# Hybrid encoder layer: attention weights left unscaled until the head pair is done, and the last linear-attention q and k columns computed as seven-product units

## The chip, the cores and the metric

One core of one Trainium2 chip. The metric is device time in microseconds (us) for one call of the layer, lower is better. The kernel before takes 2159.4 us, the median of three runs (2157.53 to 2160.07).

## What is computed

One layer over 512 tokens of width 2048, in float32. The parts that the change touches:

```
h = rmsnorm(x); proj = h @ w_in        # columns: aq ak av (1024 each), gq gk (512 each), gv gr (1024 each), 32 gate columns
# group A, 16 heads x 64: three (window, dilation) patterns, T5 bias, merged by their softmax denominators
logits = q @ k.T * 64**-0.5 + bias;  p = exp(logits - max);  s = sum(p);  o = p @ v / s
# group B, 4 heads, dk 128, dv 256: bidirectional gated linear attention on gq, gk, gv, then a norm and a swish gate gr
x = x + concat(A, B) @ w_out
x = x + (silu(h2 @ w_gate) * (h2 @ w_up)) @ w_down;  rmsnorm
```

At 512 tokens the three patterns and their merge are one softmax over all 512 keys, with a bias that holds the log of how many patterns reach a distance.

## The kernel before

Every large product is made in split precision: each operand is rounded to a `fp32r` high part (on ScalarE) and the remainder is kept as a low part (a subtraction on VectorE), and three matmuls are summed (high by high, high by low, low by high). There are two ways to do a product. A **job** (`run_job`, L311 on) does it plainly: 512 output columns, 16 slices of the contraction, and for each slice four PSUM banks by three 128x512 matmuls, twelve in all; kind "A" (L337 to L339) has the features on the partitions, kind "B" (L346 to L348) the tokens. A **unit** (`Feed.products`, `Front`) does 256 output columns in 2x2 blocks with seven block products instead of eight (the sums of blocks are made on VectorE). A unit has four pieces; a piece has seven products, and each of them two matmuls of 128x512 (L1562) and two of 128x256 (L1548). `evac7` then puts the seven results together with nine copies on ScalarE, seven additions of 256 columns and one of 512 on VectorE and four adding DMAs; `finish` multiplies by the row of reciprocal norms and writes to DRAM.

The program is written out in one order and each engine has its own queue, served strictly in that order. The order around the change:

1. Two jobs for the attention's v columns.
2. `Front`: 14 units, for the gate gr (4), the lower half of gq and gk (2), and the attention's q and k (8). q and k go to DRAM (`qkd`) and are read back per pair of heads by `read_qk` and rounded by `load_qk`.
3. Three jobs: job A for the upper half of gq and gk (`evac_gqk`, L849), then the two gv jobs.
4. Three half jobs of `w_out` (the rows that belong to attention), one whole job of `w_out`, then the rest of `w_out`, the SwiGLU units and the down projection.

In stages 3 and 4 the attention and then the gated linear attention (`gla`) run **beside** the jobs. They are generators in the list `side`. After each bank's three matmuls a job adds its rate (`RATES`, steps per slice) to a credit, and for each whole credit one step of the first generator in `side` is put into the program; `urgent` generators get one step before it. `attention` (L711) takes two steps for each unit u (a head's 128 queries; 64 units, 8 to a pair of heads). The first step of u has the scores of u (two matmuls, L630, L631) and the ScalarE work: the round of an earlier unit (L670) and the exponential of u-1 (L648), which also sums it. The second step has TensorE's transposes (L662), the products with v (L686, L687) every second unit, and on VectorE the remainder (L676), the bias and maximum of u (L640) and the sum of the two halves of the result (L705). Between the exponential and the transposes `att_norm` (L651, L653) takes the reciprocal of the sum on VectorE and scales the unit's 128x512 weights there for even u; `att_scale` (L657) does it on ScalarE for odd u. The result of a pair (`mixf`) is rounded (L738) and its remainder is taken (L751); the `w_out` half jobs read it as `mixh`.

PSUM has eight banks. The running job holds four; the scores, transposes and v products share the other four, and a bank is handed out again in the order in which it was given back (`Slots`, first in, first out), so a matmul that opens a bank waits for the VectorE instruction that read it last.

## Time and profile before

| | us |
|---|---|
| median of three runs | 2159.4 |
| the profiled execution | 2159.02 |
| its span in the profile | 2157.2 |
| stage 2, `Front`, 14 units (first L1562 to the first L337) | 104.2 to 378.0 |
| attention, first L630 to the last L687 | 399.0 to 609.8 |
| TensorE's granted clock | 1.00 of full speed |

In the profile's groups each line names engine, operation, tiles, count, busy time and the mean of one, and then the idle time of the engine just before these instructions with its releaser. PE is the matmul row of TensorE and PEld its weight loads. Matmuls overlap, so the distance between the starts of two of them says what one costs; its duration does not. In a timeline row the first number is the start, the second the length.

### The profile page before, as it was taken

The numbers are of one execution on the slowest core, as the hardware profiler recorded it, in microseconds if no ns is written. First come the engines' busy times: TensorE is split into PE (matmuls) and PEld (weight loads), VectorE is DVE, ScalarE is ACT, GpSimd is POOL, SyncE is SP. The second block draws the span as 40 slices with busy tenths as digits, with TensorE's granted clock in tenths as the row PEclk, the third lists the DMA queues.
The fourth block names the chain that finished last, engine by engine and source line by source line (L and its number), as shares of the span: only waits on it lengthen the run. The fifth ranks groups of instructions, "written<-read, shape, count | busy, mean of one in ns | idle before, by whom it ended". The sixth has DMA issues, their size and how long they took to land.

```text
span 2157.2 us, 35082 instructions
## 1 busy us (share of the span) xinstructions
PE 2145.5 (99%) x12714; PEld 1896.6 (88%) x12714; DVE 1843.6 (85%) x3187; ACT 1234.4 (57%) x2250; POOL 364.0 (17%) x501
## 2 busy tenths in 40 slices
PE   9999999999999999999999999999999999999998
PEld 7888888888888889888888888888888899999987
DVE  6699999688878788899999998999989888888885
ACT  8455555578876456455555555555555655555562
POOL 0011222211121110022112211221122220021300
PEclk9999999999999999999999999999999999999999
DMA  6367778846575863567677667776677885576982
GB/s 203 136 181 182 179 179 192 245 143 190 174 220 172 279 243 103 149 181 182 181 179 196 173 183 182 178 194 174 180 188 181 260 212 178 179 183 156 282 309 78
DMA packets 266203, 407.55 MB, mean 189 GB/s; under 512 B 19309, under 2 KB 163613, under 8 KB 266030
## 3 DMA queue, kind: packets, MB, share of 16 engines
q1 hardware_dynamic: 206238, 274.59, 39.8%
q0 software_dynamic: 59472, 130.19, 27.1%
q8 instruction: 100, 1.64, 0.3%
q14 instruction: 73, 0.60, 0.1%
q10 hardware_dynamic: 320, 0.53, 0.1%
HBM read 287.47 MB, written 66.39 MB: 164 GB/s over the span
## 4 chain that ended last, share of the span: by engine, by line
PE 56%; DMA 1%; issue 1%; DVE 1%; POOL 0%; ACT 0%; DVEq 0%; ACTq 0%; POOLq 0%
PE ps L1562 25%; PE ps L1548 12%; PE ps L1926 5%; PE ps L1927 5%; PE ps L1925 5%; PE ps L346 1%; PE ps L348 1%; PE ps L347 1%; PE ps L2122 1%; PE ps L2121 1%; PE ps L2120 1%; DMA gd<-b 1%; DMA b<-a 0%; POOL xd L1806 0%; DVE b L1471 0%
## 5 line engine op out<-in xcount | busy, mean ns | idle before, releaser
L1466 ACT CAST b<-b 128x1024 fp32r<-128x1024 f32 (+1 forms) x585 | 533.8, 944 | 386.4 <-DVE b L1471 193.1
L1471 DVE TENSOR_TENSOR b<-b,b 128x1024 fp32r<-128x1024 f32 (+1 forms) x585 | 614.0, 1084 | 34.4 <-ACT b L1466 22.9
L1562 PE MATMUL ps<-b,b 128*128 128x512 f32 x1708 | 500.7, 393 | 0.4 <-ACT b L1466 0.2
L1562 PE MATMUL ps<-a,b 128*128 128x512 f32 x1428 | 418.7, 393 | 0.3 <-DVE b L1582 0.2
L1562 PEld LDWEIGHTS ps<-b,b 128*128 128x128 f32 x1708 | 289.4, 188 | 32.6 <-ACT b L1466 0.6
L1548 PEld LDWEIGHTS ps<-b,b 128*128 128x128 f32 x1708 | 280.6, 190 | 40.8
L1548 PE MATMUL ps<-b,b 128*128 128x256 f32 x1708 | 307.4, 280 | 0.0
L1548 PEld LDWEIGHTS ps<-a,b 128*128 128x128 f32 x1428 | 236.9, 189 | 38.0 <-DVE b L1471 0.5
L1562 PEld LDWEIGHTS ps<-a,b 128*128 128x128 f32 x1428 | 238.5, 188 | 24.1 <-issue 0.6
L1548 PE MATMUL ps<-a,b 128*128 128x256 f32 x1428 | 256.6, 280 | 0.1
L1453 DVE TENSOR_TENSOR b<-b 128x512 f32<-128x512 f32 x268 | 183.6, 685 | 19.0 <-PE ps L1927 7.3
L1926 PE MATMUL ps<-b,b 128*128 128x256 f32 x624 | 176.6, 283 | 0.0
L1927 PE MATMUL ps<-b,b 128*128 128x256 f32 x624 | 176.6, 283 | 0.0
L1925 PE MATMUL ps<-b,b 128*128 128x256 f32 x624 | 176.6, 283 | 0.0
L346 PE MATMUL ps<-b,b 128*128 128x512 f32 x332 | 133.8, 403 | 0.1
L348 PE MATMUL ps<-b,b 128*128 128x512 f32 x332 | 129.8, 391 | 0.1
L347 PE MATMUL ps<-b,b 128*128 128x512 f32 x332 | 129.5, 390 | 0.0
L1454 DVE TENSOR_TENSOR b<-b,b 128x256 f32<-128x256 f32 x268 | 114.0, 425 | 9.3
L1455 DVE TENSOR_TENSOR b<-b,b 128x256 f32<-128x256 f32 x268 | 114.0, 425 | 9.2
L1927 PEld LDWEIGHTS ps<-b,b 128*128 128x128 f32 x624 | 119.8, 192 | 0.0
L1925 PEld LDWEIGHTS ps<-b,b 128*128 128x128 f32 x624 | 119.8, 192 | 0.0
L1926 PEld LDWEIGHTS ps<-b,b 128*128 128x128 f32 x624 | 119.8, 192 | 0.0
(308 smaller groups left out, 4039.8 us busy)
## 6 DMA issues: line engine op xcount, KB each, us to landing
b<-in_w_gate_dram SPq DMA_DIRECT2D x109, 512.0 KB, 3.7
b<-in_w_up_dram SPq DMA_DIRECT2D x88, 512.0 KB, 3.8
b<-in_w_down_dram SPq DMA_DIRECT2D x88, 512.0 KB, 5.4
b<-in_w_in_dram SPq DMA_DIRECT2D x86, 512.0 KB, 3.8
b<-a POOLq DMA_DIRECT2D x168, 256.0 KB, 4.5
b<-in_w_out_dram SPq DMA_DIRECT2D x32, 512.0 KB, 6.3
gd<-b POOLq DMA_DIRECT2D x22, 512.0 KB, 4.0
b<-gd SPq DMA_DIRECT2D x22, 512.0 KB, 8.3
```

Source lines behind the costliest of these rows:

```text
L346: mm(o, xh.t[:, c], wh.t[:, w], start=first and not on, stop=False, skip_group_check=on)
L347: mm(o, xh.t[:, c], wl.t[:, w], start=False, stop=False, skip_group_check=on)
L348: mm(o, xl.t[:, c], wh.t[:, w], start=False, stop=last, skip_group_check=on)
L1453: dve.tensor_tensor(s_[:, :, 0:2], r[:, :, 1:3], r[:, :, 0:1].to_broadcast(shape), op=OP.add)
L1454: dve.tensor_tensor(s_[:, :, 2], s_[:, :, 0], r[:, :, 2], op=OP.add)
L1466: act.copy(o, src)
L1471: dve.tensor_tensor(o, src, h, op=OP.subtract)
L1548: mm(o, wl, xh, start=False, stop=end, skip_group_check=True)
L1562: mm(o.rearrange("p (s t) -> p s t", s=2), wh, x_, start=first and p == 0, stop=False, skip_group_check=True)
L1925: mm(o, xh[:, t], wh, start=first and h == 0, stop=False, skip_group_check=True)
L1926: mm(o, xh[:, t], wl, start=False, stop=False, skip_group_check=True)
L1927: mm(o, xl[:, t], wh, start=False, stop=last, skip_group_check=True)
```

## The change

- **Softmax unscaled.** `att_norm` and `att_scale` are gone: the transposes and the v products use exp(.) without its reciprocal. The eight sums of a pair of heads are kept in eight columns of `small`. At the pair's end `reciprocals` turns them with one TensorE transpose (8x128, L655), takes the reciprocals on VectorE (8x128, L656), `sums_out` writes them to DRAM on POOL's queue (L660), `rows_in` reads them back twice, spread over 64 partitions each (L665, same queue), and `scaled` multiplies the pair's 128x512 result on VectorE (L670). The steps of a unit come one unit (two steps) earlier, and the round and remainder of the pair's result one unit later. The loop is one unit longer.
- **All gq and gk as units.** Job A and `evac_gqk` are gone. `Front` has 16 units: the upper half of gq and gk are units 6 and 7. So two jobs, not three, run beside the attention's first part, and their rate is 4.4 steps per slice, not 3.1. What hung on job A (`gstart`, `before_first`) hangs on the first gv job.
- **Reads spread.** `read_qk` issues its eight DMAs one in a step from the pair's first unit on, not in one burst at the second; the gate's operands (`scan_operands`, at u = 43, not 47) likewise.

```diff
-            act.activation(L.t, L.t, AF.Exp, scale=-1.0, bias=am[u % 4], accum_out=asum[u % 4])
-        def att_norm(u):
-            dve.reciprocal(ar[u % 4], asum[u % 4])
-            if u % 2 == 0:
-                dve.tensor_scalar(AT[u].t, AT[u].t, ar[u % 4], None, op0=OP.mult)
-        def att_scale(u):
-            if u % 2:
-                act.activation(AT[u].t, AT[u].t, AF.Copy, scale=ar[u % 4])
+            act.activation(L.t, L.t, AF.Exp, scale=-1.0, bias=am[u % 4], accum_out=asum[:, u % 8:u % 8 + 1])
+        def reciprocals():
+            b = ps.get()
+            pe.transpose(b.t[0:8, 0:P], asum, idn)
+            dve.reciprocal(inv, b.t[0:8, 0:P])
+            put(b)
+        def sums_out(pr):
+            pool.dma_start(out=rd[pr], in_=inv)
+            rows[pr] = s2.get()
+        def rows_in(pr, n):
+            src = rd[pr, 4 * n:4 * n + 4].rearrange("j p -> (j p)")[None]
+            pool.dma_start(out=rows[pr].t[64 * n:64 * n + 64], in_=src.to_broadcast([64, 512]))
+        def scaled(pr):
+            v = lambda o: o.t.rearrange("p (b c) -> p b c", c=P)
+            f, r = mixf[pr], rows.pop(pr)
+            dve.tensor_tensor(v(f), v(f), v(r)[:, :, ::-1], op=OP.mult)
+            put(r)
...
-            for u in range(UNITS + 7):
+            for u in range(UNITS + 8):
...
-                run(att_scale, u - 3)
-                run(att_round, u - 4)
+                run(att_round, u - 3)
                 run(att_exp, u - 1)
...
                 yield
-                run(att_norm, u - 2)
-                run(att_transpose, u - 3)
+                next(reads, None)
+                run(att_transpose, u - 2)
+                if u % 2:
+                    run(att_av, (u - 5) // 2, UNITS // 2)
+                run(att_rest, u - 3)
+                run(att_max, u)
                 if u % 2 == 0:
-                    run(att_av, (u - 6) // 2, UNITS // 2)
-                run(att_rest, u - 4)
-                run(att_max, u)
-                if u % 2:
-                    run(att_mix, (u - 7) // 2, UNITS // 2)
+                    run(att_mix, (u - 6) // 2, UNITS // 2)
+                if pr >= 0 and s_ == 0:
+                    reciprocals()
...
+                if pr >= 0 and s_ == 6:
+                    scaled(pr)
...
-        RATES = (3.1, 4.0)
+        RATES = (4.4, 4.0)
-        job("A", [piece512(seg, None, k) for k in range(0, KT, 2)], list(range(KT)), acts_h,
-            evac_gqk, rate=RATES[0], start=gstart, before=before_first, limit=3)
...
                 self.units = [(w_in, C_GR + g * 256) for g in range(4)] + [(w_in, C_GQ), (w_in, C_GK)] + \
+                    [(w_in, C_GQ + 256), (w_in, C_GK + 256)] + \
                     [(w_in, c + g * 256) for g in range(4) for c in (C_AQ, C_AK)]
```

How this stands in the engines' queues, at one place: the boundary between the fourth and the fifth pair of heads. TensorE before, from the fifth pair's first scores (L630; `ps` is a PSUM bank with its number, L346 to L348 are a job's matmuls, L662 the transposes, L686 and L687 products with v):

```order
L630 MATMUL ps4_214_5233<-a29_269_5099,a14_268_5098 128x512
L631 MATMUL ps4_214_5233<-a22_257_4980,a14_268_5098 128x512
L346 MATMUL ps0_176_4675<-a26_266_5081,b3_38_444 128x512
L347 MATMUL ps0_176_4675<-a12_267_5082,b3_38_444 128x512
L348 MATMUL ps0_176_4675<-a26_266_5081,b3_38_444 128x512
L346 MATMUL ps6_173_4672<-b32_501_5138,b4_41_477 128x512
L347 MATMUL ps6_173_4672<-b32_501_5138,b4_41_477 128x512
L348 MATMUL ps6_173_4672<-b32_501_5138,b4_41_477 128x512
L662 MATMUL ps1_215_5255<-idn_71,a20_274_5152 128x128 x4
L686 MATMUL ps2_216_5260<-b18_503_5164,b26_452_4065 128x256
L687 MATMUL ps2_216_5260<-b30_504_5165,b26_452_4065 128x256
```

TensorE now, from the same scores (L633; the transposes are L676 now, L655 is the transpose of the eight sums):

```order
L633 MATMUL ps7_233_5492<-a11_263_5368,a35_262_5367 128x512
L634 MATMUL ps7_233_5492<-a1_250_5212,a35_262_5367 128x512
L346 MATMUL ps4_218_5324<-a30_258_5330,b13_14_215 128x512
L347 MATMUL ps4_218_5324<-a18_259_5331,b13_14_215 128x512
L348 MATMUL ps4_218_5324<-a30_258_5330,b13_14_215 128x512
L676 MATMUL ps1_234_5503<-idn_71,a25_271_5440 128x128 x4
L655 MATMUL ps3_235_5512<-idn_71,small_76 8x128
L346 MATMUL ps5_219_5325<-a30_258_5330,b13_14_215 128x512
L347 MATMUL ps5_219_5325<-a18_259_5331,b13_14_215 128x512
L348 MATMUL ps5_219_5325<-a30_258_5330,b13_14_215 128x512
L633 MATMUL ps7_236_5519<-a11_263_5368,a35_262_5367 128x512
L634 MATMUL ps7_236_5519<-a1_250_5212,a35_262_5367 128x512
```

The transpose of the sums has come in behind the unit's own transposes; it opens bank ps3, which a unit's transposes (ps3_231) held before it, and the next scores open ps7 straight after the scores before them. With a rate of 4.4 there are fewer of a job's matmuls between two steps over the whole stage.

VectorE before, from the maximum of the fourth pair's last unit (L640, 128x512; L588 the low part of the next pair's k, L705 as above, L218 a job's remainder of weights):

```order
L640 ISA a2_281_5225,small_76<-ps1_212_5206,b19_494_5016 128x512
L640 ISA small_76 128x1
L705 TENSOR_TENSOR a10_282_5227<-ps2_211_5186,a6_280_5211 64x2x128
L588 SCALAR_TENSOR_TENSOR a25_258_4981<-a25_258_4981,a18_271_5101 128x512
L218 TENSOR_TENSOR a19_279_5201<-b12_491_4913,a5_278_5200 128x512
L651 RECIPROCAL small_76<-small_76 128x1
L653 TENSOR_SCALAR a4_277_5196<-a4_277_5196,small_76 128x512
L676 TENSOR_TENSOR b14_506_5238<-ps5_213_5219,b28_505_5237 128x4x128
```

VectorE now, from the same maximum (L643; L777 is the remainder of the pair's result, L589 the low parts of the next pair's q and k, L690 a unit's remainder, L656 the new reciprocal):

```order
L643 ISA a16_275_5473,small_76<-ps1_230_5448,b28_544_5277 128x512
L643 ISA small_76 128x1
L777 TENSOR_TENSOR a19_274_5456<-a20_242_5160,a7_273_5455 128x512
L218 TENSOR_TENSOR a6_268_5393<-b30_532_5039,a29_267_5392 128x512
L589 SCALAR_TENSOR_TENSOR a12_264_5369<-a31_249_5211,a12_264_5369 64x512
L589 SCALAR_TENSOR_TENSOR a34_251_5213<-a34_251_5213,a22_265_5370 128x512
L690 TENSOR_TENSOR b29_554_5452<-ps3_231_5458,b18_553_5451 128x4x128
L643 ISA a13_281_5509,small_76<-ps7_233_5492,b9_552_5420 128x512
L643 ISA small_76 128x1
L719 TENSOR_TENSOR a26_272_5442<-ps0_232_5463,a0_280_5497 64x2x128
L656 RECIPROCAL wrow1_72<-ps3_235_5512 8x128
L690 TENSOR_TENSOR b16_558_5523<-ps1_234_5503,b32_557_5522 128x4x128
```

The single reciprocals (L651) and the scaling (L653) are gone. The remainder of the third pair's result (L777) stands one unit later than it did, and with it and two subtractions for q and k (L589) there are now four instructions between the last unit's maximum and the remainder (L690) that gives bank ps3 back; the reciprocal of the eight rows follows behind.

73 lines of the change are left out of this document (38 added, 35 removed).

## Prediction

> **What bounds the kernel now.** I read the page's busy shares first, then its slices, then windows of two stages, then the start-to-start distances of matmuls in the timeline.
>
> ```profile
> PE 2145.5 (99%) x12714; PEld 1896.6 (88%) x12714; DVE 1843.6 (85%) x3187; ACT 1234.4 (57%) x2250; POOL 364.0 (17%) x501
> ...
> PEclk9999999999999999999999999999999999999999
> ...
> PE 56%; DMA 1%; issue 1%; DVE 1%; POOL 0%; ACT 0%; DVEq 0%; ACTq 0%; POOLq 0%
> ```
>
> ```profile
> 150.00:200.00 50.00, 50.00 (x291) 44.04 (x290) 47.13 (x74) 26.18 (x43) 11.67 (x14) 1.00 0.77 188
> 450.00:500.00 50.00, 50.00 (x283) 42.73 (x283) 42.82 (x103) 39.36 (x85) 13.10 (x26) 1.00 0.58 170
> ```
>
> TensorE is busy 99% of the span at the full granted clock, and the chain that ended last is TensorE wherever it names an engine with more than 1%. A busy PE need not be a dense one, since durations overlap, so below I price a matmul by the distance of starts. The two windows (columns: stretch, PE, PEld, VectorE, ScalarE, POOL, clock, DMA) are `Front` and the attention stage: PE full in both, VectorE at 47.1 and 42.8 of 50, ScalarE at 39.4 of 50 in the second. So the kernel's time is the sum of what TensorE has to issue, and a saving on VectorE or ScalarE is worth nothing by itself. It matters only where such an engine makes TensorE wait, and VectorE is near enough for that.
>
> **Job A for two units.** The timeline gives both prices. These are the first and the last matmul of `Front`'s stretch, and one slice of a job:
>
> ```profile
> 104.24 0.62 PE L1562 MATMUL ps<-b,b 128*128 128x512 f32 x2
> ...
> 377.95 0.40 PE L337 MATMUL ps<-b,b 128*128 128x512 f32 x1
> ...
> 380.68 0.39 PE L825 MATMUL ps<-b,a 128*64 128x512 f32 x1
> ```
>
> From 377.95 to 380.68 lie the twelve matmuls of one slice of job A: 2.73 us, 0.2275 each. The job has 16 slices, so 43.7 us go. `Front`'s 14 units take 377.95 - 104.24 = 273.7 us, 19.55 each, with their waits; two more add 39.1 us. The net is **-4.6 us**. The weights are read either way (8 pieces of 512 KB). What job A asked of VectorE and ScalarE beside the attention (16 remainders, 16 rounds, 4 evacuations) goes into `Front`, where VectorE is 94% busy at the same TensorE pace as before; I count the two units' waits by the mean above and nothing more.
>
> **The normalisation.** These are groups of the stretch 420 to 622 on VectorE and one on ScalarE (count, busy, mean ns, then idle before):
>
> ```profile
> L676 DVE TENSOR_TENSOR b<-ps,b 128x512 fp32r<-128x512 f32 x60 | 41.0, 684 | 9.0 <-ACT b L670 8.5
> L640 DVE CUSTOM_DVE_ANT_0 a<-ps,b 128x512 f32<-128x512 f32 x56 | 38.4, 685 | 14.1 <-PE ps L631 14.1
> L218 DVE TENSOR_TENSOR b<-b,b 128x512 fp32r<-128x512 f32 x26 | 17.5, 687 | 2.1 <-ACT b L237 1.9
> L653 DVE TENSOR_SCALAR a<-a,small 128x512 f32<-128x512 f32 x29 | 14.1, 487 | 1.0
> L705 DVE TENSOR_TENSOR a<-ps,a 64x256 f32<-64x256 f32 x31 | 13.0, 420 | 3.0 <-ACT a L696 2.5
> L651 DVE RECIPROCAL small<-small 128x1 f32<-128x1 f32 x57 | 8.9, 157 | 0.3
> L588 DVE SCALAR_TENSOR_TENSOR a<-a,a 64x512 fp32r<-64x512 f32 x12 | 8.3, 689 | 0.6 <-ACT a L592 0.4
> L640 DVE DVE_READ_ACCUMULATOR2_ANT small<- 128x1 f32 x56 | 4.6, 83 | 0.0
> L751 DVE TENSOR_TENSOR a<-a,a 128x512 fp32r<-128x512 f32 x5 | 3.4, 686 | 0.0
> L880 DVE TENSOR_SCALAR b<-ps,small 128x512 f32<-128x512 f32 x4 | 3.0, 750 | 3.9 <-PE ps L348 3.9
> L657 ACT ACTIVATE a<-a,small 128x512 f32<-128x512 f32 x29 | 20.9, 719 | 3.4 <-DVE small L651 3.3
> ```
>
> Removed on VectorE: 64 x 0.157 + 32 x 0.487 = 25.6 us; on ScalarE 32 x 0.72 = 23 us. No TensorE time hangs on it: the only wait of the attention's matmuls over 0.2 us is this one (the last bracket is idle time and releaser), behind the evacuation of a gv job:
>
> ```profile
> 526.88 0.39 PE L348 MATMUL ps<-a,b 128*128 128x512 f32 x1
> 527.43 0.66 PE L662 MATMUL ps<-idn,a 128*128 128x128 f32 x4 [0.17 <-DVE b L880]
> ```
>
> So its removal saves TensorE 0. Added: eight transposes of the sums on TensorE. The nearest form is the 128x128 transpose, four of which stand from 472.31 to the next start in the rows below, 0.35 us with the change of mode: 0.09 to 0.35 each, and I take 0.11, since each stands directly behind other transposes: **+0.9 us** (0.7 to 2.8). On VectorE eight multiplications of 0.685 (L751's form) and eight reciprocals of 8x128. No row has that form: between 0.157 (one column, L651) and 0.685 (512 columns, L640); I take 0.3, nearer the small end since it has a quarter of the columns. [...]
>
> **The attention against two jobs.** This is where a gain can go.
>
> ```profile
> 471.15 0.40 PE L630 MATMUL ps<-a,a 128*128 128x512 f32 x1
> 471.39 0.39 PE L631 MATMUL ps<-a,a 128*128 128x512 f32 x1
> 471.61 0.40 PE L346 MATMUL ps<-a,b 128*128 128x512 f32 x1
> ...
> 472.31 0.60 PE L662 MATMUL ps<-idn,a 128*128 128x128 f32 x4
> 472.66 0.36 PE L686 MATMUL ps<-b,b 128*128 128x256 f32 x1
> ...
> 473.70 0.40 PE L346 MATMUL ps<-a,b 128*128 128x512 f32 x1
> ```
>
> Per unit: scores 0.46, transposes 0.35, half of the v products (1.04 / 2), and about 0.09 for the first matmul after a change of mode: 1.4 us. The order has 534 job matmuls between the first scores and the last v products before, 378 now: 534 x 0.2275 + 64 x 1.4 = 211 us (the table's 399.0 to 609.8 says 210.8), and 378 x 0.2275 + 64 x 1.4 + 0.9 = **176.5 us** now. VectorE's work in it, from the rows: 64 x (0.685 + 0.083 + 0.684) + 32 x 0.42 + 28 x 0.687 (low parts of q and k) + 7 x 0.686 = 130 us in both. Before there come 25.6 of normalisation, some 46 remainders of weights (31.5) and evacuations, 7 or so: 194 of 211, 92%. Now there come 36 remainders (24.7), 7 x 0.685 + 8 x 0.3, and 5 of evacuation: **167 of 176.5**, 95%. VectorE's spare time shrinks from 17 to 9.5 us.
>
> Where would TensorE notice? At the place that the order shows. VectorE starts a maximum 0.63 us after its scores at best (471.39 + 0.39 - 471.15). From the last unit's maximum to the end of the remainder that gives bank ps3 back: 0.63 + 0.685 + 0.083 + 0.686 + 0.687 + 2 x 0.687 + 0.684, and 0.1 for the signal, 4.9 us. TensorE comes from those scores to the transpose of the sums over 6 job matmuls (1.37), scores twice (0.92), transposes twice (0.7), one set of v products (1.04): 4.0 us. So it stands there about 0.9 us. At the other boundaries the order puts 9 job matmuls between (4.7 us) and two to four instructions on VectorE: two more come out at 4.9 against 4.7, the rest below. In sum **+1.4 us**. Before, the bank that such a remainder gave back was wanted only by scores some 7 us behind, and nothing stood there. The transpose also needs the last exponential (0.73 us, one unit ahead), which is done earlier by this count. Elsewhere the pace per unit falls from 3.3 to 2.75 us while VectorE's slowest stretch (rounding q and k, multiplication, remainder) grows by one instruction: I take 0.5 us of waits, which the 0.5 us of now (526.88 to 527.43 and what follows) pays for. So 0 there, between -0.5 and +10 (below).
>
> **DMA and the tail.** On POOL the last two reads of the next pair's q and k now stand behind a DMA that waits for the sums to land, some 2 to 5.5 us by the rows below; their first reader stands two units (5.5 us) and more behind, so I count nothing. Each pair's sums make a trip: out by POOL, back twice, then the multiplication on VectorE, which stands in its queue before the work of every later step.
>
> ```profile
> a<-qkd POOLq DMA_DIRECT2D x64, 128.0 KB, 5.5
> ...
> a<-in_gla_gate_w_fwd_dram POOLq DMA_DIRECT2D x1, 32.0 KB, 1.9
> ```
>
> By these rows 0.3 + 1.9 + 5.5 and three issues of 0.55 make 9.4 us. The multiplication stands six units later: 16 us while the scores run, hidden. For the last pair no scores are left, and its six units last only 36 job matmuls and two sets of v products, 10.7 us: hidden by about 1 us, and if it is not, VectorE stands up to 5 us with three or more slices of weights ready; I take 0, at most +3. [...]
>
> The gated linear attention starts later against the jobs: by the order its last transposes stand 15 job matmuls before the `w_out` matmul that needs the result, where they stood 45 before.
>
> ```profile
> 744.03 1.04 PE L1132 MATMUL ps<-idn,b 128*128 128x128 f32 x8
> 747.39 1.29 DVE L922 TENSOR_TENSOR b<-a,b 128x512 fp32r<-128x512 f32 x2
> ```
>
> The first remainder ends about 748.05, 4.0 us after the transposes start. TensorE would need 1.0 + 15 x 0.2275 + 0.45 (the low part is read by the third matmul) = 4.8 us. Hidden by 0.8; at most +2.
>
> **Sum:** -43.7 + 39.1 + 0.9 + 1.4 + 0 = -2.3 us. The profiled execution took 2159.0 us, 0.4 below the median of 2159.4; the forecast is **2156.8**. About 0.2% (4.3 us) is what a measurement of this kernel can tell from no change, so this counts as the same.
>
> **Rivals.**
> - *No new wait at all.* TensorE's sum alone: -43.7 + 39.1 + 0.9, and the 0.5 us of waits gone as well: -4.2, 2154.8; with some of the waits of the linear attention gone too, 2153. For it: ScalarE loses 23 us in the stage, and a unit's transposes no longer wait for a reciprocal. Against it: the count of 4.9 against 4.0. 0.27.
> - *VectorE becomes the bound of the attention stage*, and the kernel is slower. In the rows above it idles 14.1 + 9.0 + 3.0 + 2.1 us before work that TensorE or ScalarE hands it, 28 us with 57 units in the stretch, 32 for 64. That idle time is order, not lack of work: the maximum waits for scores. Only 9.5 us of it fit into 176.5. If 20 us of it stay, the stage lasts 187 us, 10.5 over my sum less what I counted: about 2166. It outweighs the gain from 13 us of idle time on (-4.6 + 0.9 + 167 + 13 - 176.5 = 0). [...] 0.2.
> - *The units do not save.* With VectorE at 47 of 50 us two more units could each add a wait as the stage has (0.3), and a late trip of the last sums 3: about 2160.3 (-2.3 + 0.6 + 3), within 0.2%. 0.08, and 0.45 for the forecast itself.
>
> So faster by over 0.2% (below 2155.1) 0.27, within 0.2% 0.53, slower 0.2. The range takes in the first rival and most of the second: 2153 to 2165.
>
> **What would show it.** `Front`'s first L1562 to the first L337: 312.8 us. First scores to last v products: 177 to 179 us, with idle time before the new transposes released by VectorE's remainder, about 0.9 us at the boundary of the fourth and fifth pair. The multiplication must have no idle time before it that a DMA ended. The forecast is wrong if the stage takes over 183 us (second rival), or if new waits appear in `Front` or before the `w_out` matmuls.

## The result, and the profile after

The changed kernel takes **2172.7 us**, the median of six runs (2168.99 to 2174.73), against 2159.3 (2157.53 to 2160.45, six runs): a ratio of 1.0061, with a 95% interval of 1.0048 to 1.0074. It is 13.2 us slower by the ratio (10.4 to 16.0), where 2.6 us faster was forecast, and lies outside the range. The profiled execution took 2174.73 us, the longest of the six and 15.7 more than that of before, so what the trace adds up to is to be held against 15.8 and not against 13.2. Its busy shares, from the page:

```profile
PE 2149.2 (99%) x12754; PEld 1898.5 (87%) x12754; DVE 1855.2 (85%) x3145; ACT 1226.1 (56%) x2236; POOL 382.2 (18%) x531
```

The page looks as before: TensorE is 99% busy. The loss is 0.7% of the span, and a busy share rounds it away. The matmul row of the timeline shows the stages, by the first matmul of `Front`, the first job matmul, the first scores and the last product with v:

```profile
104.26 0.62 PE L1575 MATMUL ps<-b,b 128*128 128x512 f32 x2
...
417.86 0.40 PE L346 MATMUL ps<-b,b 128*128 128x512 f32 x1
...
435.39 0.39 PE L633 MATMUL ps<-a,a 128*128 128x512 f32 x1
...
621.79 0.28 PE L701 MATMUL ps<-b,b 128*128 128x256 f32 x1
```

| stage | before | after | difference | matmuls of jobs gone, at 0.2275 | so waits and additions |
|---|---|---|---|---|---|
| `Front` | 273.7 | 313.6 | +39.9 | | +39.9 (two units) |
| to the first scores | 21.1 | 17.5 | -3.6 | 15: -3.4 | -0.2 |
| first scores to last v products | 210.8 | 186.4 | -24.4 | 156: -35.5 | **+11.1** |
| behind it, to the span's end | 1547.4 | 1551.2 | +3.8 | 21: -4.8 | **+8.6** |
| the span | 2157.2 | 2173.0 | +15.8 | 192: -43.7 | |

So the two units cost what was forecast of them, and 19.7 us came up in two stretches, the attention stage and what lies behind it. The waits of TensorE name three places there (what waited, for which instruction, us in total, times, the longest):

```profile
PE ps L346 <- DVE a L972: 4.9, 2, 4.1
PE ps L700 <- DMA b<-vd: 2.6, 1, 2.6
PE ps L655 <- DVE b L690: 2.4, 3, 1.2
...
PE ps L655 <- ACT a L710: 1.0, 1, 1.0
PE ps L655 <- ACT b L684: 0.8, 1, 0.8
```

**1. Behind the stage: the last pair's trip.** The timelines of POOL, VectorE, ScalarE and TensorE, in this order:

```profile
617.18 0.51 POOL L660 DMA_DIRECT2D rd<-wrow  x1 [7.12 <-DVE wrow L656]
622.44 1.10 POOL L665 DMA_DIRECT2D a<-rd  x2 [4.75 <-PE ps L701]
```

```profile
615.95 0.94 DVE L656 RECIPROCAL wrow<-ps 8x128 f32<-8x128 f32 x1
...
630.91 0.69 DVE L670 TENSOR_TENSOR a<-a,a 128x512 f32<-128x512 f32 x1 [6.92 <-DMA a<-rd]
...
640.91 0.75 DVE L972 TENSOR_SCALAR a<-ps,wcol 128x512 f32<-128x512 f32 x1 [6.38 <-ACT a L969]
```

```profile
631.64 0.62 ACT L758 CAST b<-a 128x512 fp32r<-128x512 f32 x1 [8.52 <-DVE a L670]
...
632.80 1.28 ACT L174 ACT_TABLE_LOAD   x1
634.09 2.19 ACT L928 ACTIVATE a<-a 128x512 f32<-128x512 f32 x4
636.19 2.17 ACT L928 ACTIVATE b<-b 128x512 f32<-128x512 f32 x4
...
640.19 0.69 ACT L969 ACTIVATE a<-ps,wcol 128x512 f32<-128x512 f32 x1
```

```profile
637.18 0.39 PE L348 MATMUL ps<-b,a 128*128 128x512 f32 x1
641.72 0.79 PE L346 MATMUL ps<-b,a 128*128 128x512 f32 x1 [4.14 <-DVE a L972]
642.31 0.63 PE L347 MATMUL ps<-b,a 128*128 128x512 f32 x1
642.73 0.63 PE L348 MATMUL ps<-b,a 128*128 128x512 f32 x1
...
650.25 0.39 PE L348 MATMUL ps<-b,a 128*128 128x512 f32 x1
```

Read from the first: the reciprocals end at 616.9, the sums go out at 617.18, and the first read back is issued at 622.44. Its row names a product with v, but what POOL's queue waited for ahead of it came at 621.9 (the view of its line), and that is the landing of the sums: the longest of such a DMA was 4.7 us, and 617.18 + 4.7 is 621.9. The multiplication starts at 630.91: **14.0 us for the trip**, half of it with VectorE idle (6.92). That alone would not have stopped TensorE, which had matmuls to issue until 637.4. But ScalarE's round of the pair (L758) stood still with it, and behind the round stand, in ScalarE's strict order, a table load, eight silus of the gate (634.09 to 638.36), a cast of weights, another table load and L969. L969 and L972 read the gate product's bank, and the next `w_out` job opens that bank (the order shows the wait at the job's matmul). The 18 matmuls from 637.18 to 650.25 took 13.07 us, and at 0.2275 each 4.1: **9.0 us lost**. About 5.3 are standing, and the rest is the clock: from 642.31 on two starts lie 0.43 us apart, where 0.23 is usual.

**2. In the stage: the bank of the transposed sums.** The boundary of the fourth and fifth pair, TensorE's timeline and then VectorE's:

```profile
522.24 0.60 PE L676 MATMUL ps<-idn,a 128*128 128x128 f32 x4
524.04 0.27 PE L655 MATMUL ps<-idn,small 128*8 128x128 f32 x1 [1.21 <-DVE b L690]
```

```profile
520.58 0.68 DVE L777 TENSOR_TENSOR a<-a,a 128x512 fp32r<-128x512 f32 x1
521.18 0.68 DVE L218 TENSOR_TENSOR a<-b,a 128x512 fp32r<-128x512 f32 x1
521.89 1.41 DVE L589 SCALAR_TENSOR_TENSOR a<-a,a 64x512 fp32r<-64x512 f32 x2
523.22 0.68 DVE L690 TENSOR_TENSOR b<-ps,b 128x512 fp32r<-128x512 f32 x1
```

L655 opens the bank that the remainder L690 reads last, and L690 stands behind two low parts of q and k (L589). L655 waits in this way at five of the seven boundaries inside the stage, three times for VectorE and twice for ScalarE: 4.2 us idle by the waits, and some 5 by the distance of starts. (What became of these 5 us when the bank was taken away stands with that experiment.)

**3. In the stage: v comes late.** The second half of v is read at the same units as before (u = 34 to 36), while the products with it come a unit earlier and each unit is shorter:

```profile
538.03 0.28 PE L701 MATMUL ps<-b,b 128*128 128x256 f32 x1
540.88 0.50 PE L700 MATMUL ps<-b,b 128*128 128x256 f32 x1 [2.58 <-DMA b<-vd]
...
541.40 0.63 PE L633 MATMUL ps<-a,a 128*128 128x512 f32 x1
541.83 0.63 PE L634 MATMUL ps<-a,a 128*128 128x512 f32 x1
```

Again the matmuls behind it are 0.43 apart; with that this place costs some 4.9 us. The last quarter of v was issued at 531.7 and landed 9.1 us later, where it took 4.3 before (the views of its line). The DMA queues between its issue and its landing, in the change and then before (packets, MB, share of the 16 DMA engines' time; q0 holds the DMAs that POOL issues, q1 those of SP, v's among them):

```profile
q1 hardware_dynamic: 462, 1.39, 53.2%
q0 software_dynamic: 380, 1.03, 49.0%
```

```profile
q1 hardware_dynamic: 296, 1.07, 77.4%
```

Before, POOL's queue moved nothing in that time: its reads of q and k had all been issued 12 us and more ahead. In the change they are issued from 526.5 to 532.9, since they are spread over the steps and stand in POOL's queue behind the sums' DMA (L660 at 525.98, ahead of which POOL stood 12.30 us for the reciprocals). Together with the reads of the sums they take half of the DMA engines' time just when v is on its way. No run moved these reads alone, so this cause is argued and not shown. But it fits in all ten runs with the faster pace whose read of v stands at these units: where POOL's share was 13 to 31% (mended, units_only, mended_end, recip_bank, two_fix), the quarter landed in 4.2 to 5.9 us, and where it was 35 to 57% (held, last_pe, the change, short43, norm7), in 7.4 to 10.2.

The granted clock (the third number from the end) of two windows with a long stand. The page's own row of clocks shows 9 in all 40 slices, since one slice is 54 us long and hides such a dip:

```profile
536.00:546.00 10.00, 7.42 (x34) 6.09 (x33) 5.60 (x13) 5.36 (x14) 0.00 (x0) 0.83 0.71 215
634.00:652.00 18.00, 13.09 (x41) 9.71 (x40) 10.44 (x20) 15.37 (x29) 5.79 (x10) 0.72 0.35 68
```

Added up: 9.0 behind the stage, where the table has 8.6; in it 5, 4.9, 0.9 for the transposes themselves and 0.4 for scores that wait for L690 (516.15), 11.2, where the table has 11.1. This says where the time stood in this one execution; what of it goes with which cause, only the runs can say.

### The profile page after: what moved, and what is told of

It is laid out like the page before. It is cut to its first block, busy times and chain, and to the rows that moved or that the text cites. A ratio compares the mean times of both kernels' runs of the same rounds, so it can differ in the third digit from the quotient of the medians.

```text
span 2173.0 us, 35256 instructions
## 1 busy us (share of the span) xinstructions
PE 2149.2 (99%) x12754; PEld 1898.5 (87%) x12754; DVE 1855.2 (85%) x3145; ACT 1226.1 (56%) x2236; POOL 382.2 (18%) x531
## 4 chain that ended last, share of the span: by engine, by line
PE 58%; DVE 0%; DMA 0%; issue 0%; ACT 0%; DVEq 0%; ACTq 0%
PE ps L1575 24%; PE ps L1561 12%; PE ps L1942 5%; PE ps L1941 5%; PE ps L1940 5%; PE ps L347 1%; PE ps L346 1%; PE ps L348 1%; PE ps L2137 1%; PE ps L2136 1%; PE ps L2135 1%; DMA gd<-b 0%; DVE b L1484 0%; DVE a L2168 0%; DVE a L1595 0%
## 5 line engine op out<-in xcount | busy, mean ns | idle before, releaser
L1479 ACT CAST b<-b 128x1024 fp32r<-128x1024 f32 (+1 forms) x601 | 548.6, 944 | 407.8 <-DVE b L1484 210.2
L1484 DVE TENSOR_TENSOR b<-b,b 128x1024 fp32r<-128x1024 f32 (+1 forms) x601 | 630.6, 1084 | 34.1 <-ACT b L1479 22.1
L1575 PE MATMUL ps<-b,b 128*128 128x512 f32 x1760 | 517.3, 393 | 0.4 <-ACT b L1479 0.2
L1575 PE MATMUL ps<-a,b 128*128 128x512 f32 x1488 | 436.5, 393 | 0.6 <-ACT b L1479 0.4
L1575 PEld LDWEIGHTS ps<-b,b 128*128 128x128 f32 x1760 | 298.1, 188 | 33.2 <-ACT b L1479 0.7
L1561 PEld LDWEIGHTS ps<-b,b 128*128 128x128 f32 x1760 | 289.9, 190 | 42.3
L1561 PE MATMUL ps<-b,b 128*128 128x256 f32 x1760 | 318.0, 280 | 0.0
L1561 PEld LDWEIGHTS ps<-a,b 128*128 128x128 f32 x1488 | 246.5, 189 | 39.6 <-DVE b L1484 1.0
L1575 PEld LDWEIGHTS ps<-a,b 128*128 128x128 f32 x1488 | 248.9, 188 | 25.9 <-issue 0.6
L1561 PE MATMUL ps<-a,b 128*128 128x256 f32 x1488 | 267.7, 281 | 0.1
L1940 PE MATMUL ps<-b,b 128*128 128x256 f32 x624 | 176.6, 283 | 0.0
L1941 PE MATMUL ps<-b,b 128*128 128x256 f32 x624 | 176.6, 283 | 0.0
L1942 PE MATMUL ps<-b,b 128*128 128x256 f32 x624 | 176.6, 283 | 0.0
L346 PE MATMUL ps<-b,b 128*128 128x512 f32 x352 | 142.4, 404 | 0.3 <-ACT b L455 0.3
L348 PE MATMUL ps<-b,b 128*128 128x512 f32 x352 | 137.9, 392 | 0.2 <-DVE b L459 0.2
L347 PE MATMUL ps<-b,b 128*128 128x512 f32 x352 | 137.7, 391 | 0.0
L1467 DVE TENSOR_TENSOR b<-b,b 128x256 f32<-128x256 f32 x276 | 117.4, 425 | 9.6
L1468 DVE TENSOR_TENSOR b<-b,b 128x256 f32<-128x256 f32 x276 | 117.4, 425 | 9.5
L1620 POOL DMA_DIRECT2D b<-a x58 | 50.2, 866 | 411.4 <-ACT b L1479 267.0
L1940 PEld LDWEIGHTS ps<-b,b 128*128 128x128 f32 x624 | 119.8, 192 | 0.0
L1941 PEld LDWEIGHTS ps<-b,b 128*128 128x128 f32 x624 | 119.8, 192 | 0.0
```

What stands on the lines that cost most here:

```text
L346: mm(o, xh.t[:, c], wh.t[:, w], start=first and not on, stop=False, skip_group_check=on)
L347: mm(o, xh.t[:, c], wl.t[:, w], start=False, stop=False, skip_group_check=on)
L348: mm(o, xl.t[:, c], wh.t[:, w], start=False, stop=last, skip_group_check=on)
L1467: dve.tensor_tensor(s_[:, :, 2], s_[:, :, 0], r[:, :, 2], op=OP.add)
L1479: act.copy(o, src)
L1484: dve.tensor_tensor(o, src, h, op=OP.subtract)
```

## The experiments

Each is the changed kernel with the edit shown, unless said otherwise, timed against the kernel before on the same chip. All compute the whole layer. "Over before" is worked out from the ratio at 2159 us. The traces below are of one execution of each run.

| run | median us | ratio, 95% interval | over before, us |
|---|---|---|---|
| the change | 2172.7 | 1.0061 (1.0048 to 1.0074) | +13.2 |
| softmax_only: softmax part alone | 2169.1 | 1.0043 (1.0029 to 1.0057) | +9.3 |
| units_only: unit part alone | 2163.5 | 1.0013 (1.0004 to 1.0022) | +2.8 |
| v_early: v read earlier | 2172.9 | 1.0064 (1.0050 to 1.0078) | +13.8 |
| last_pe: last pair spread by TensorE | 2167.7 | 1.0039 (1.0025 to 1.0052) | +8.4 |
| recip_bank: sums into the result bank | 2168.8 | 1.0046 (1.0032 to 1.0059) | +9.9 |
| all3: these three together | 2164.2 | 1.0022 (1.0013 to 1.0031) | +4.7 |
| two_fix: the last two of the three | 2162.3 | 1.0012 (1.0004 to 1.0021) | +2.6 |
| soft_two: these two, softmax part alone | 2165.9 | 1.0028 (1.0017 to 1.0039) | +6.0 |
| held: these two, gv buffers held | 2167.4 | 1.0037 (1.0023 to 1.0051) | +8.0 |
| short43: these two, pace 2% slower, earlier end | 2163.4 | 1.0019 (1.0010 to 1.0027) | +4.1 |
| norm7: last pair as before | 2166.4 | 1.0031 (1.0020 to 1.0043) | +6.7 |
| mended: norm7 and another bank | 2161.7 | 1.0012 (1.0004 to 1.0021) | +2.6 |
| mended_soft: mended, softmax part alone | 2162.6 | 1.0014 (1.0006 to 1.0023) | +3.0 |
| mended_end: mended, attention ends earlier | 2165.2 | 1.0025 (1.0015 to 1.0035) | +5.4 |

The theory after the traces: the loss is three separate waits that the softmax part brings (the trip, the bank, v), made worse by the granted clock, which went to 0.50 at two of them (541.00 to 544.41 and 639.98 to 650.22). The rival: VectorE is short of time in the denser stage, as the second rival of the prediction had it, so that a wait taken away comes back elsewhere.

**The two parts alone.** The units on the kernel before (job A gone, rate 4.4), and the softmax part, spread reads included, without them (job A back, rate 3.1).

```diff
 units_only, on the kernel before:
-        RATES = (3.1, 4.0)
+        RATES = (4.4, 4.0)
-        job("A", [piece512(seg, None, k) for k in range(0, KT, 2)], ...)
+                    [(w_in, C_GQ + 256), (w_in, C_GK + 256)] + \
 softmax_only, on the change: the same lines the other way round
```

> The kernel before with only the second part of the change: job A gone, two more seven-product units, two jobs at 4.4 steps per slice; the softmax is scaled unit by unit as before. Theory: TensorE issues 4.6 us less, but VectorE has 167 - 8 + 26 = 185 us of work in an attention stage of 176 us of TensorE, so the stage grows by 9 us or more: 2163 to 2170 us. Rival (the faster pace itself is harmless, only the new steps of the unscaled softmax cost): 2155 to 2157 us.

> The changed kernel without its second part: job A is back, three jobs at 3.1 steps per slice, 14 units; the softmax is unscaled with the trip through DRAM. Theory (three places): the last pair's trip costs nearly as much as in the changed kernel, since its six units are as short (5 to 10 us), the late v and the bank wait cost less at the slower pace (0 to 3 us): 2165 to 2172 us. Rival (VectorE bounds the stage in the changed kernel): here VectorE has 20 us to spare, so the time is within 2 us of 2160.

+2.8 and +9.3, in sum 12.1 of 13.2: the parts nearly add, and both times are their theories'. But the theory of units_only had 185 us of VectorE work and 9 us or more on its stage, and neither came. The units save 4.6 us by the forecast's count and yet lose. Their stage, first scores to last v products, took 181.2 us with 384 job matmuls; the kernel before has 534 and took 210.8, and 150 matmuls less are 34.1, so 176.7 was to be had: 4.5 us of new waits, which the pace brings without any of the softmax part. The largest is 1.6 us, the transposes' wait for the odd units' weights that ScalarE scales. (The trace is of an execution of 2160.2 us, 3.3 below the run's median, so it shows the lesser part of the loss.) The rival, that VectorE is short of time, can be read from the same stage: its row of the change and of units_only (the third time behind the stretch is VectorE's).

```profile
435.39:621.79 186.40, 179.22 (x1026) 152.00 (x1025) 154.52 (x317) 138.66 (x304) 48.63 (x93) 0.99 0.66 195
```

```profile
435.59:616.80 181.21, 178.85 (x1024) 150.57 (x1023) 165.30 (x399) 157.64 (x336) 38.49 (x72) 1.00 0.64 190
```

VectorE did 10.8 us more in units_only, and the stage was 5.2 us shorter, with six job matmuls more in it. In the change VectorE stood idle for 31.9 us of the 186.4. So the sum of its work is not what makes the stage long; that single instructions of it come late at the faster pace is another matter, and the waits show it.

The softmax part left the stage at 210.3, so its 9 us lie behind it. The trip is there again, 12.9 us from the end of the reciprocals at 602.6 (VectorE's timeline):

```profile
615.57 0.69 DVE L670 TENSOR_TENSOR a<-a,a 128x512 f32<-128x512 f32 x1 [3.81 <-DMA a<-rd]
```

Behind it the linear attention's transposes (L1066) stand 3.31 us for VectorE, which waits 2.13 us for a memset on POOL. How much of the 9.3 us hangs on the trip, this run alone does not say.

**v read four units earlier.**

```diff
-                if 34 <= u < 37:
-                    load_v(1, ((0,), (1,), (2, 3))[u - 34])
+                if 30 <= u < 33:
+                    load_v(1, ((0,), (1,), (2, 3))[u - 30])
```

> The changed kernel with one edit: the second half of v is read from DRAM four units earlier (u = 30 to 32, not 34 to 36). Theory (three separate places): the products with v of the ninth head no longer wait (2.7 us of idle time and about 2.2 us at the lower clock behind it), so about 4.9 us less than the changed kernel: 2168 us; the waits before the transposes of the sums (5 us) and before the first w_out matmuls (about 10 us) stay. Rival (VectorE bounds the whole attention stage): the idle time only moves to the next wait, the time stays within 1 us of the changed kernel's 2172.7.

No gain. The wait for v is gone and one as long stands 20 us ahead of it. VectorE's timeline, then TensorE's:

```profile
518.46 0.69 DVE L690 TENSOR_TENSOR b<-ps,b 128x512 fp32r<-128x512 f32 x1 [4.20 <-DMA gvd<-b]
```

```profile
519.20 0.50 PE L633 MATMUL ps<-a,a 128*128 128x512 f32 x1 [2.53 <-DVE b L690]
```

The remainder needs a buffer from which a gv result is still being written to DRAM. The buffers go round in the order in which they came free, so an earlier read of v takes the free ones, and the next taker waits for a DMA. Here the theory's "taken away, it is gone" was wrong, and the rival's kind of result came; but what came back is a buffer, not VectorE's time: VectorE stood idle for 4.20 us. From the scores of unit 36 to those of unit 40, where the wait for v was, this run is 4.5 us shorter than the change, and ahead of that 3.7 longer (the table below).

**The last pair without a trip.** First with eight small matmuls that spread the reciprocals over the partitions, into a bank that the multiplication reads; later, since these took TensorE 1.5 us (619.82 to 621.33 in two_fix), with the last pair normalised as in the kernel before, which adds nothing on TensorE.

```diff
 last_pe:
+        def spread(pr):
+            b = rows[pr] = ps.get()
+            for j in range(8):
+                w = idn[0:8, j:j + 1].to_broadcast([8, 64])
+                mm(b.t[j // 4 * 64:j // 4 * 64 + 64, j % 4 * P:(j % 4 + 1) * P], w, inv, start=True, stop=True)
-                if pr >= 0 and s_ == 1:
+                if 0 <= pr < 7 and s_ == 1:
                     sums_out(pr)
+                if pr == 7 and s_ == 5:
+                    spread(pr)
 norm7:
+                if u - 2 >= UNITS - 8:
+                    run(att_scale, u - 2)
+                if u - 1 >= UNITS - 8:
+                    run(att_norm, u - 1)
```

> The changed kernel with one edit: the last pair's reciprocals are spread over the partitions by eight small TensorE matmuls into a PSUM bank, without the trip through DRAM; the other seven pairs as in the changed kernel. Theory (three places): VectorE does not stand 6.9 us before the last multiplication, ScalarE does not stand 8.5 us, the gate's Silu and the weights' rounding are in time, so the 5.5 us of idle time and 4 us of lower clock at 637 to 650 us go, for about 1 us of matmuls: about 2164 us. Rival (VectorE bounds the stage): the stage before is as long, and ScalarE's Silu and table loads still delay the weights, so less than 3 us is gained: 2170 us.

> The changed kernel, but the last pair is normalised as in the kernel before (a reciprocal per unit on VectorE, the weights scaled on VectorE and ScalarE in turn), so it makes no trip through DRAM, and TensorE gets nothing in its place. Theory: the trip's wait and the low clock behind it were 9 to 10 us, of which some comes back as other waits: 2163 to 2167. Rival: other waits take all of what the trip cost: 2170 or more.

4.8 and 6.5 us of the 13.2 are gone, so the trip is a cause, though less came back than the 9.0 us that the trace has there. The window that had TensorE busy 13.09 of 18 us at a clock of 0.72, in norm7:

```profile
634.00:652.00 18.00, 18.00 (x87) 15.08 (x86) 15.55 (x30) 11.32 (x23) 7.85 (x12) 1.00 0.80 205
```

TensorE is full at the full clock, so the 9.0 us are gone from there. In norm7's trace what lies behind the stage takes 1542.1 us, against 1551.2 in the change: 9.1 less, and the stage is as long as it was (186.5). So the trip is worth what the trace of the change shows; the medians show 6.5, since the execution of the change that was profiled lay 2.0 above its median. With the spread the stage lasts 189.0, as v comes later still there (a wait of 3.6 us).

**The sums into a bank that is open anyway.** The transposes go into unused columns of the result bank, ahead of the addition that gives it back.

```diff
-            b = ps.get()
-            pe.transpose(b.t[0:8, 0:P], asum, idn)
-            dve.reciprocal(inv, b.t[0:8, 0:P])
-            put(b)
+            o = OT[(u - 6) // 2][0].t[0:8, 256:256 + P]
+            pe.transpose(o, asum, idn)
+            dve.reciprocal(inv, o)
```

> The changed kernel with one edit: the transpose of the sums writes into the unused half of the PSUM bank that holds the last products with v, and takes no bank of its own. Theory: the waits of 0.3 to 1.4 us before it go (5 us in eight pairs), because they are waits for the bank's last reader on VectorE and not for the sums: about 2168 us. Rival: TensorE waits there for VectorE's backlog in general, and the next scores or transposes wait instead: within 1.5 us of the changed kernel's 2172.7.

3.3 us are gone, the stage falls to 181.5 us, and of 4.2 us of waits before L655 one is left (0.9, for ScalarE). But the wait for v is gone as well, though nothing of it was touched, and that is nearly the whole gain. The scores of unit 36 start at 533.58 in the change and at 533.24 here, those of unit 40 so (the change, then this run):

```profile
548.35 0.40 PE L633 MATMUL ps<-a,a 128*128 128x512 f32 x1
```

```profile
543.58 0.40 PE L633 MATMUL ps<-a,a 128*128 128x512 f32 x1
```

The stage in three parts, by the starts of scores and the last product with v:

| run | unit 0 to 36 | 36 to 40, with the wait for v | 40 to the end of the stage |
|---|---|---|---|
| the change | 98.2 | 14.8 | 73.4 |
| v_early | 101.9 | 10.3 | 73.8 |
| recip_bank | 97.7 | 10.3 | 73.4 |
| two_fix | 96.7 | 10.3 | 73.4 |
| norm7 | 99.6 | 11.5 | 75.4 |
| mended | 96.6 | 11.4 | 76.4 |

Outside the place of v the bank's edit gave 0.5 us, with the boundaries of the pairs all in these two stretches: what TensorE no longer stood before L655 came back as other waits (scores for L689, 1.1 us, and smaller ones). So the time is the theory's and the reason is not: at the boundaries the rival of this run came out, and the bank is not shown to be a cause of the loss. Nor did the edit mend v by design. The last quarter was issued at 531.4, as in the change, and landed in 5.5 us, beside less of POOL's traffic: POOL stood 2.88 us before its reads of the sums, so these and the reads behind them were issued from 530.85 on, in the change from 528.09. The edit was not meant to do that; that v was mended by it is luck.

**All three, and two of them.**

> The changed kernel with the three edits of v_early, last_pe and recip_bank together. Theory (three separate places): the losses add, 4.9 + 9 + 5 us, so 2172.7 - 19 = about 2154 to 2156 us, faster than the kernel before by the 4.6 us that the two units save less the new transposes. Rival (VectorE bounds the attention stage, 167 us of work in 176): the stage stays at 183 us or more, and the time is 2163 us or more.

> Both parts, with the trip and the bank mended, and the second half of v read where the change has it. Theory: the wait for v was a consequence (the sums' bank delayed VectorE, the slots and so the read), it stays away, and the time is that of the kernel with all three edits, 2163 to 2165. Rival: the wait for v of about 3 us and the low clock behind it come back: 2167 or more.

The three together miss the theory (2154 to 2156) by 8 us. The time is the rival's (2163 or more), its stage is not: 181.5 us, where the rival had 183 or more. Without the earlier v the kernel is no slower (2162.3, even below what either expectation had), and v lands in 5.9 us there: two edits do what three did. The theory's reason for it, a read that the bank had delayed, does not hold: the read was issued at 531.2, in the change at 531.7. What is left in its waits is small and spread over several pairs of engines; the longest is a transpose of the sums that now waits for ScalarE.

**The two edits on the softmax part alone.** (The unit part taken out of two_fix.)

> The softmax part alone (job A back, rate 3.1), with the last pair's reciprocals spread by eight small matmuls and the sums transposed into the result bank. It cost +9.6 us as it was. Theory: that cost is the last pair's trip through DRAM (5 us by itself) and the bank of the transposes (3.9 us by itself), so 2159 to 2162. Rival: it is the new order of a unit's steps, one unit earlier, whatever the trip and the bank do: 2165 or more.

Only 3.3 of 9.3 us came back, less than the theory asked; the rival's bound (2165) is just passed. But its stage lasts 210.7 us, with six job matmuls less than before (1.4 us) and with the transposes of the sums, so the new order inside the stage costs little there. Two places behind it explain most of the 6.0: the spread's 1.5 us, and a wait of the linear attention. Its timeline, VectorE and then TensorE:

```profile
642.29 0.72 DVE L1079 COPY_PREDICATED a<-masks,ps 128x512 f32<-128x512 uint32 x1 [2.14 <-POOL a L1068]
...
643.06 0.66 PE L1073 MATMUL ps<-idn,a 128*128 128x128 f32 x4 [1.76 <-DVE a L1079]
```

**Buffers held, and a slower pace,** both on two_fix.

```diff
 held:
-                        put(v)
+                        kept.append(v)
-                    put(rb.pop(1))
+                    put(rb.pop(1), *kept)
 short43:
-        RATES = (4.4, 4.0)
+        RATES = (4.3, 4.0)
-            for u in range(UNITS + 8):
+            for u in range(UNITS + 6):
 and for the last pair spread at s_ == 3, scaled at 4, rounded at 5 (were 5, 6, 7)
```

> As two_fix, but the buffers in which a gv job's result is written out are given back only at the first w_out half job, so no unit's low part waits for that DMA. Theory: the wait at the first gv job's end (1.3 us of TensorE in the kernel with all three edits) goes and nothing takes its place: 2162 to 2163. Rival: with two buffers fewer in the ring another tile waits for its buffer: 2164 or more.

> As two_fix, but the last pair, which has no trip any more, is done two units earlier (four steps fewer) and the rate is 4.3 steps per slice for 4.4, so the attention ends at nearly the same place of the program at a pace 2% slower. Theory: what is left is the density of the attention's stage (VectorE 95% busy), so slack gives 1 to 3 us: 2161 to 2163. Rival: what is left are single places with late buffers, which do not feel the pace: 2164 to 2165.

The theory on the buffers fell, and the time is the rival's. Holding up to four took away VectorE's wait for them (1.7 us in two_fix) and the wait for v came back, longer (3.41 us, with 0.43 between the matmuls behind it); the stage is 5.0 us longer:

```profile
539.44 0.52 PE L705 MATMUL ps<-b,b 128*128 128x256 f32 x1 [3.41 <-DMA b<-vd]
...
539.97 0.63 PE L633 MATMUL ps<-a,a 128*128 128x512 f32 x1
540.40 0.63 PE L634 MATMUL ps<-a,a 128*128 128x512 f32 x1
```

The rival's reason, a tile that waits for its buffer, is not shown by this: the last quarter of v was issued at 529.65, not later than in two_fix (531.2), and took 9.7 us to land, where it took 5.9. The slower pace came out between its two expectations, and gained nothing on two_fix (2163.4 against 2162.3, intervals that overlap). The run alone decides nothing, since it also ends the attention four steps earlier, which cost 2.8 us where it was tried by itself (mended_end below). Its stage says a little more: 182.5 us with six job matmuls more than two_fix, whose stage takes 180.5, so 0.6 longer for its work. The slower pace took no waits out of the stage.

**Mended.** norm7 with the sums in 16 columns, so that they can be transposed one unit later, into the result bank; without the units; and with an end four steps earlier.

```diff
 mended, beside the edits of norm7 and recip_bank:
-        asum = small[:, 60:68]
+        asum = small2[:, 0:16]
-                if pr >= 0 and s_ == 0:
-                    reciprocals()
+                if 0 <= pr < 7 and s_ == 1:
+                    reciprocals(u)
 mended_soft: the unit part taken out.  mended_end, on mended:
-            for u in range(UNITS + 8):
+            for u in range(UNITS + 6):
```

> As norm7, and the sums are kept in 16 columns and transposed one unit later, into the result bank of the pair that is being done, so that this transpose waits for no exponential and for no bank. Theory: with the trip, the bank and the exponential gone, the attention's stage has under 3 us of waits over those of before: 2158 to 2161. Rival: waits move to late buffers as in the earlier runs: 2163 or more.

> As mended, without the unit part (job A back, rate 3.1). Theory: the softmax part is worth nothing and costs nothing once its three waits are gone, 2159.5 to 2161. Rival: the new order of the steps costs by itself: 2163 or more.

> As mended, but the last pair's result is rounded two units earlier and the attention ends four steps earlier, so the linear attention starts that much earlier beside the jobs. Theory: its start was hidden already (by 0.8 us in the forecast), so this changes under 1 us against mended. Rival: its late start costs 1 to 3 us, which this gives back.

The first two miss their theories by 0.7 and 1.6 us and stay short of the rivals: +2.6 and +3.0. So the softmax part, freed of its trip and its bank, costs little more than its transposes and some waits, and gains nothing. With the units the stage still takes 184.4 us, with waits of scores for a bank that VectorE gives back:

```profile
PE ps L634 <- DVE b L700: 3.5, 4, 1.2
```

The earlier end made it slower, +5.4, which neither expectation had: among the new waits are 1.8 us in the linear attention, which mended does not have. A shift of four steps, with nothing else changed, moved this kernel by 2.8 us. No version beat the kernel before; two_fix and mended come within 2.6 us of it. The spread reads were never tried alone.

## Why the prediction was wrong, point by point

- **Job A for two units: right.** -43.7 is what the order says; the two units took 39.9 us against 39.1 (`Front` 313.6 us, 312.8 forecast): 0.8 for both, where the third rival allowed 0.6.
- **The normalisation's removal saves TensorE 0: right.** **The transposes of the sums: right in size**; with no wait before it, 0.78 us lie between the unit's transposes and the second job matmul behind them (614.89 to 615.67), and 0.67 in the kernel before, which has no transpose of sums there (463.12 to 463.79): some 0.1 us each, the waits before them aside.
- **The reciprocals: the size was wrong.** Taken as 0.3 us, between 0.157 and 0.685; measured 0.935, outside both ends (group of VectorE in the stage: count, busy, mean ns, idle before):

```profile
L656 DVE RECIPROCAL wrow<-ps 8x128 f32<-8x128 f32 x8 | 7.5, 935 | 0.0
```

  The 5 us more of VectorE are no term of the loss: in the waits shown, only 0.6 us of the last trip hang on them.
- **Waits at the boundaries, +1.4: the mechanism was right, the size wrong.** At the fourth and fifth pair 0.9 was forecast and 1.2 of idle time came, for the remainder behind the low parts, as described. (For the signal, 0.1 in the sum without a row, 0.14 stand between the end of L690 at 523.90 and L655.) But it came at five boundaries and not three, twice behind ScalarE (L710, L684), which the count left out: some 5 us. They are no cost of the bank by itself: taking it away gave 0.5 us outside the place of v, and units_only, which has neither that transpose nor its bank, has 4.5 us of waits in its stage. What the sum put at "0 there" for the faster pace elsewhere in the stage is about this size.
- **Other waits of the stage, 0: wrong.** v was not priced at all. Its read was not in the diff, and that was the error: what reads it was moved a unit ahead and a unit made a sixth shorter, while its issue stayed, and other reads were moved beside it. From the issue of the last quarter to the last of the first products that need it were 8.9 us before (508.64 to 517.50); in the change the product that waited would have started 6.4 us behind the issue (538.15), and the read took 9.1. With the clock this cost 4.9 us by the trace's own distances, 4.5 against the runs without the wait. The sum counted only what the spread reads' first readers need, and nothing of whom these reads run beside.
- **The last pair's trip "hidden by about 1 us", 0 and at most +3: wrong, the step that failed by most.** Three things in it. The trip was 14.0 us, not 9.4: the landings were taken from medians of other DMAs (1.9 and 5.5), and here the sums took 4.7 (to 621.9) and the last read 7.9 (from its issue at 623.0 to the multiplication at 630.9). The cover was not 10.7 us from the transposes of the sums, because VectorE ended the reciprocals only at 616.9 and was out of other work at 624.0 (630.91 less 6.92): 7.1. And the loss was bounded by VectorE's idle time, when the instruction that waits behind L670 stands on ScalarE, with a dozen others queued behind it and a bank at their end: 9.0 us, with the clock, where the term had 0. The runs without a trip got 4.8 and 6.5 back in the whole, and norm7's trace 9.1 behind the stage.
- **The linear attention's late start, 0: right for the change**; no matmul of the linear attention stands among its waits of 0.2 us and more. In the variants such waits came and went (1.8 us in soft_two).
- **Rivals.** "VectorE becomes the bound" gave 187 us for the stage and 2166 in all; the stage took 186.4. That its number for the stage held is luck: 4.5 us of it are the wait for v, a DMA; and in all the kernel came out 7 us above its 2166, for the trip. Its sum of work is refuted by units_only, with more of it in a shorter stage; its other half, that instructions come late at the faster pace though VectorE has idle time, fits the 4.5 us of waits there. Its price was wrong too, since it summed VectorE's durations (0.68) where starts that follow at once lie 0.60 apart (520.58 and 521.18 above): VectorE was busy for 154.5 us of the stage, not 167, and of 176.5 us 22 would have been left and not 9.5. For TensorE I had gone by starts, for VectorE not. "The units do not save" allowed 3 us for a late trip; it cost 9.0.
- **Slips of the sum.** The boundaries come to 0.9 + 0.2 + 0.2, 1.3 and not 1.4; 36 job matmuls and two sets of v products last 10.3 us, not 10.7; 2.3 less than 2159.0 is 2156.7. None of these decides anything.
- **"The multiplication must have no idle time before it that a DMA ended"** was the right sign: 6.92 us.

What stays open: what brings POOL's reads beside v's, that they are spread or that they stand behind the sums' DMA, and which of the stage's small waits the faster pace brings. The kernels with units were in the stage for 180.5 to 189 us, and none near 176.5; which order or how many buffers would bring it there was not found.

## What to carry to other kernels

A reduction that is put off to the end of a block has its full latency at the last block, where no work covers it: follow that one trip alone, with the landings under load, to every engine whose queue stands behind its end. When a stage gets shorter, or a queue of reads gets a new wait in it, ask of each load in it whether its issue moved too and what now runs beside it, whether it is in the diff or not. When an edit takes away a wait and time comes back, look where in the stage it came back: here it was another wait's. And price a long wait of TensorE with the clock that goes with it: the two here, with 0.50 granted at and behind them, cost 1.7 times the time that the matmuls stood (9.0 us for 5.3, 4.5 for 2.6).

## What the runs showed of the hardware

- **The clock fell at stands of 2.53 to 4.14 us.** Stands of 2.58 and 3.41 us (idle time in the rows above) were followed at once by matmuls 0.43 us apart, where 0.23 is usual; the stand of 1.21 (524.04) was not (1.00 granted from 523 to 534). In v_early the clock fell not right behind the stand of 2.53 us but 1.1 us later, in the midst of running matmuls, and was back some 3.4 us after that (520.24 to 523.6) (TensorE's timeline):

```profile
520.00 0.40 PE L347 MATMUL ps<-b,b 128*128 128x512 f32 x1
520.24 0.58 PE L348 MATMUL ps<-b,b 128*128 128x512 f32 x1
...
523.17 0.63 PE L634 MATMUL ps<-a,a 128*128 128x512 f32 x1
523.60 0.65 PE L676 MATMUL ps<-idn,a 128*128 128x128 f32 x4
```

  In the change it was granted at 0.50 from 541.00 to 544.41, 3.41 us, and at the trip from 639.98, while TensorE stood, to 650.22, 10.24 us, three times as long. In v_early the mean granted from 519 to 523 was 0.66, and in held the starts are 0.43 apart from 539.97 to 542.11. What sets when the clock falls and how long it stays there, no run shows.
- **Landings under load.** In the change 4 KB took 1.9 us in the median and 4.7 at most, and reads of 128 KB (64 partitions from one row) 3.3 to 7.8. The last 512 KB of v took 9.1 with 49.0% of the DMA engines' time taken by POOL's queue, and 4.3 in the kernel before with none of it.
- **The reciprocal of 128 columns (8x128, from PSUM) took 0.935 us**, that of one column (128x1, from SBUF) 0.157, where a subtraction of 512 columns (128x512, from PSUM) took 0.68.
